# One core, a planned schedule: spread memsets, own weight tiles for two early products, another estimate for early transfers, systems in four transfers

## The chip, the cores and the metric

The kernel runs on 1 core of one Trainium2 chip. The metric is the time of one execution on the device in microseconds (us); lower is better. Comparisons are of medians of several runs.

## The reference

One layer of an encoder trunk on a prompt of 2048 tokens (width 1024) and a sample of 32 tokens with a cache. A combined projection feeds two branches, chunk-band attention (A) and a gated delta rule (B); both are gated, projected, merged and normalised.

```python
h = layer_norm(x, ln0_g, ln0_b)
qa, ka, va, za, qkv_b, zb, a_b, b_b, gate_a, gate_b = split_projection(h @ w_in)
ya = (chunk_band_attention(qa, ka, va, rel_bias) * silu(za)) @ w_branch_a
c = silu(causal_conv(qkv_b, conv_w));  qb, kb, vb = split(c)          # l2-normalised q and k
# per block of 64 tokens and head:
m = (k_beta @ kb.T) * decay * strict
t_inv = triangular_solve(eye + m, eye)                               # the "system"
u = t_inv @ v_beta;  w = t_inv @ (k_beta * exp(gc))
v_new = u - w @ s;  o = (q * exp(gc)) @ s + qk @ v_new               # recurrence over blocks
s = s * exp(g_last) + k_dec.T @ v_new
yb = (rms_norm(o) * silu(zb)) @ w_branch_b
y  = layer_norm(ALPHA * h + (sigmoid(gate_a) * ya + sigmoid(gate_b) * yb) @ w_out)
```

## The kernel before

**Precision and products.** Everything is float32. A product of the combined projection multiplies 128 columns of `w_in` with the normalised input, kept transposed in `hT`. Both sides are split into a half-precision part and its rest (`hi`, `lo` of the input, `whi`, `wlo` of the weights), so a block of 512 tokens takes 3 x 8 matmuls of 128x512: `whi` and `wlo` on `hi`, then `whi` on `lo`. They go to the two PSUM banks `pj`; an `evac` of each block copies the result on.

**Stages.** The 2048 tokens are worked on in two halves. For each half the products of branch B run first, then those of branch A; the gates' products fill in between. The order of the first half's products (`all_jobs`): two gates (`HEAD`), which are called products 1 and 2 here; the small product of the columns a and b (`w_ab`, 64 columns), product 3; then the convolution channels of the first pair of heads, products 4, 5 and 6, and so on; six gates (`TAIL`) close branch B's phase, and then comes branch A with its values (`vf`). Products 1 and 2 run together (`two`): their blocks of 256, 256 and 512 tokens alternate.

**The way of a weight.** `fetch` loads the raw weights into one of two tiles `wraw` (gate `raw_gate`). `divide` takes a `w_gate`, of which there are two, and with it a pair `whi`, `wlo`; the sum of squares of the weights (ACT, a small matmul `b<-w_sq` on PE, then DVE, POOL and DVE: `power`) gives a scale; ACT scales and casts, POOL subtracts. `multiply` gives the `w_gate` back behind the last block of a product.

**The way of the input.** `build_h` loads 16 tiles of 128 tokens; a tile takes statistics and a normalisation on DVE, eight transposes on PE into banks `b` and `a`, scaling on ACT and DVE, a cast on ACT (`hi`) and a subtraction on POOL (`lo`). The first 8 tiles are the first half.

**Branch B.** `phase_b` makes block-diagonal matrices (`diag`): 4 tiles `k_bd`, 4 `qk_bd`, 3 each of `q_bd`, `kd_bd`, `u_bd`, 128x1024 each, set to zero on DVE where they are made, once for each half. `worker` does the convolutions, `prep` the decays, `system` the matrices of one block of a pair of heads (8 chunks at once); it writes the systems to DRAM (`sol_p`). `solve` reads them back into `sys_p`, with one system on each row, the four groups of 32 rows holding the same 128 KB, and `substitute` solves them on DVE in 31 steps. `inverse` puts the result together, and `chain` runs the recurrence, whose matmuls go to banks `x` and `o`: 64 steps in the first half, in each of which PE and DVE take turns (`r`, `vn`, `state`).

**What sets the order.** The program is one stream of instructions for each engine. It is not written by hand: generators (`Stream`) yield at gates and marks, and a planner (`Flow`) always continues the one with the smallest planned clock. Each instruction adds a planned cost (`price`), each transfer a planned landing (`transfer`). An engine does its instructions strictly in the order so found; all that the planner estimates can change is this order. Every compute instruction is recorded at line 260 and every transfer at line 283, so the profile's rows are told apart by the names of tiles.

```python
        start = max(self.cur.clock + 0.2, self.busy.get(queue, 0.0)) + 0.5
        self.busy[queue] = start
        end = max(start + 0.6, self.busy.get("DMA", 0.0)) + size / 200e3
```

Of the kernel before, what the change touches and what calls it, by code (L numbers as in the profile page):

```python
# [56 lines left out]
for _p in range(1, NP):  # L57
    ORDER += [(_p, 0), (_p, 1), (_p, 2), (_p - 1, 3)] + [None] * FILL[_p]
ORDER += [(NP - 1, 3)]
MARGIN = 1.6  # L60
LEAD = 5.0
BLOCKS = [
    [(0, 512, 0), (512, 512, 512)],
    [(0, 512, 1024), (512, 272, 1536), (784, 272, 1808)],
# [90 lines left out]
class Flow:  # L155
# [47 lines left out]
    def transfer(self, queue, size):  # L203

        start = max(self.cur.clock + 0.2, self.busy.get(queue, 0.0)) + 0.5
        self.busy[queue] = start
        end = max(start + 0.6, self.busy.get("DMA", 0.0)) + size / 200e3
        self.busy["DMA"] = end
        return end + MARGIN

# [58 lines left out]
def trunk(ctx: ExitStack, tc: tile.TileContext, x_p, x_s, cache_k, cache_v, st_conv, st_gdn,  # L269
# [301 lines left out]
    class Job:  # L571
# [3 lines left out]
        def __init__(self, half, wid, src, evac=None, key=None, cols=P, blocks=None):  # L575
            self.wid = wid
            self.half, self.src, self.evac, self.cols, self.key = half, src, evac, cols, key
            self.end = self.two = False
            self.blocks = blocks or BLOCKS[half]

    NRAW = 2
# [41 lines left out]
    def divide():  # L623

        while True:
            job, raw, t = yield from q_raw.get()
            yield w_gate
            hi = wpool.tile([P, KD, P], F16, tag="whi", bufs=2, name="whi")
            lo = wpool.tile([P, KD, P], F16, tag="wlo", bufs=2, name="wlo")
            sc = w_scale[:, job.wid:job.wid + 1]  # L630
            yield t
            if job.half == 0:
                S.activation(out=hi[:], in_=raw[:], func=AF.Square, accum_out=w_sq[:])

                yield flow.cur.clock + (0.0 if job.wid < 34 and job.wid > 31 else 1.0)
                yield from power(sc, w_sq[:])
                flow.start(factors(job.wid))
            src, main = raw[:, :, 0:job.cols], hi[:, :, 0:job.cols]
            S.activation(out=src, in_=src, func=AF.Copy, scale=sc)
            for i in range(2):  # L640
                ks = slice(4 * i, 4 * i + 4)
                S.copy(out=main[:, ks], in_=src[:, ks])
                yield

                rest_ = lo[:, ks] if job.cols == P else hi[:, ks, job.cols:P]
                for q in range(0, 4, 2):
                    G.tensor_tensor(out=rest_[:, q:q + 2], in0=src[:, 4 * i + q:4 * i + q + 2],
                                    in1=main[:, 4 * i + q:4 * i + q + 2], op=ALU.subtract)
                if i:
                    raw_gate.give()  # L650
                    q_w.put((job, hi, lo))
                yield
# [14 lines left out]
    def multiply():  # L667

        while True:
            some, todo = [], [(0, 0)]  # L670
            while todo:
                bi, which = todo.pop(0)
                if which == len(some):
                    some.append((yield from q_w.get()))
                    job = some[which][0]
                    if which == 0:

                        todo = [(b, w) for b in range(len(job.blocks)) for w in range(1 + job.two)][1:]
                    if job.key:
                        job.open = mark()  # L680
                        flow.start(open_job(job))
                job, wh, wl = some[which]
                c0, n, gcol = job.blocks[bi]
                tiles = range(c0 // P, (c0 + n + P - 1) // P)
                for i in tiles:
                    yield h_ready[job.half][i]
                hh, hl = h_cols(job.half, c0, n)
                yield bank["pj"]
                ps = pt("pj")
                for k in range(KD):  # L690
                    PE.matmul(ps[:, 0:n], wh[:, k], hh[:, k, :], start=(k == 0), stop=False)
                    yield
                    if job.cols == P:
                        PE.matmul(ps[:, 0:n], wl[:, k], hh[:, k, :], start=False, stop=False)
                        yield
                for i in tiles:
                    yield l_ready[job.half][i]
                for k in range(KD):
                    PE.matmul(ps[:, 0:n], wh[:, k], hl[:, k, :], start=False, stop=(k == KD - 1))
                    if k == KD - 1:  # L700
                        last = bi == len(job.blocks) - 1
                        if job.end and (bi == 0 or last):
                            h_free[0 if bi == 0 else 1].give()
                        if last:
                            w_gate.give()
                    yield
                flow.start(evac(job, bi, c0, n, gcol, ps))
                if job.end and job.half == 1:
                    if last:
                        jobs_done.done()  # L710
                        flow.start(leave())
# [74 lines left out]
    def phase_b(half):  # L786
# [21 lines left out]
        def diag(name, bufs):  # L808
            ts = []
            for i in range(bufs):  # L810
                t = bp.tile([P, 8, P], F32, name=f"{name}{i}")
                V.memset(t[:], 0.0)
                ts.append(t)
            return ts

        k_bd, qk_bd = (diag(n, NPAR) for n in ("k_bd", "qk_bd"))
        q_bd, kd_bd, u_bd = (diag(n, NSIDE) for n in ("q_bd", "kd_bd", "u_bd"))
# [353 lines left out]
        def system(k):  # L1171
# [3 lines left out]
            k.par = yield from par_slots.take()  # L1175
            yield k.qk_ready
            yield k.prep
            k.pn = yield from p_slots.take()
            kb, qkb = k.kb, k.qkb = k_bd[k.par], qk_bd[k.par]
            p_c = k.p_c = p_cs[k.pn]  # L1180
# [44 lines left out]
        def solve():  # L1225
            while True:
                k, t = yield from q_sys.get()
                sys_p = bp.tile([P, 32, 32], F32, tag="sys_p", bufs=2, name="sys_p")
                sys_u = bp.tile([P, 8, 32], F32, tag="sys_u", bufs=2, name="sys_u")
                sys_t = bp.tile([P, 8, 32], F32, tag="sys_t", bufs=2, name="sys_t")  # L1230
                G.memset(sys_u[:], 0.0)
                for g in range(4):
                    G.memset(sys_u[g * 32:(g + 1) * 32].rearrange("p r i -> p (r i)")[:, g::36], 1.0)
                yield t
                p0 = pd[k.n % (2 * NP)][:]
                yield dma(sys_p[:].rearrange("p j i -> p (j i)"),
                          bass.AP(p0.tensor, p0.offset, [[0, 4], [1024, 32], [1, 1024]]))
                yield from substitute(sys_p, sys_u, sys_t)
                for g in range(4):
                    t = dma(ud[k.n % (2 * NP)][:].rearrange("s (r g i) -> g s r i", g=4, i=32)[g], sys_u[g * 32:(g + 1) * 32])  # L1240
                flow.start(inverse(k, t))
# [191 lines left out]
                return job_ab()  # L1433
            return job_conv(p, i) if i < 3 else job_z(p)

        for g in (worker(todo), worker(decays), prep(), local(), solve(), solve()):
            flow.start(g)
        for some in blocks + ([[sample]] if last else []):
            flow.start(chain(some))
# [504 lines left out]
    def marked():  # L1944

        ahead, half = [], None
        for job in all_jobs():
            if job.half != half:
                if ahead:
                    ahead[-2].two = ahead[-1].end = True  # L1950
                    yield from ahead
                ahead, half, n = [], job.half, 0
                job.two = True
            n += 1
            if n <= 2:
                if job.key is None:
                    job.blocks = FIRST[half]
                yield job
                continue
            ahead.append(job)  # L1960
            if len(ahead) > 2:
                yield ahead.pop(0)
        ahead[-2].two = ahead[-1].end = True
        yield from ahead
# [258 lines left out]
            all_done.done()  # L2223


    with ExitStack() as stack0:
        open_banks(stack0, "ps0", a=3)
        xp = stack0.enter_context(tc.tile_pool(name="x0", bufs=1, reuse_waits="tile"))
        flow.start(norm_params(xp))
        flow.start(build_h(0, xp, 8))  # L2230
        flow.start(fetch(marked()), 2.0)
        flow.start(setup(xp), 20.0)
        flow.start(setup2(xp), 30.0)
        flow.start(spread(), 100.0)
        flow.start(divide())
        flow.start(multiply())
        flow.run(l_ready[0][7])
    for half in range(2):
        stack, make, done = phase_b(half)
        enter(1, half, make)  # L2240
        flow.run(done)
        stack.close()
        if half:
            wr_pool.append(ctx.enter_context(tc.tile_pool(name="wr0", bufs=1)))
            wr_open.done()
            gp = ctx.enter_context(tc.tile_pool(name="gp", bufs=1, reuse_waits="tile"))
            for gen in (load_g(), sg_ahead(), merge()):
                flow.start(gen)
# [67 lines left out]
```

## Time and profile before

| what | value |
|---|---|
| median of 3 runs | 2083.18 us (2080.98 to 2087.81) |
| the profiled execution | 2081.13 us |
| its span | 2079.4 us |
| mean granted clock of TensorE | 0.982 |
| DVE busy | 1456.5 us (70%) |
| ACT busy | 977.0 us (47%) |
| POOL busy | 709.3 us (34%) |
| moved by DMA | 196.53 MB, mean 95 GB/s |

The profile is of one execution. PE is the matmul engine, DVE the vector engine, ACT the scalar engine, POOL the general engine, SP the queue that issues all transfers. In a row of the timeline stand the start and the duration in us, the engine, the line, the operation, what it writes and reads, and in brackets how long the engine had been idle and what ended that. In a row of a table of windows stand, for each engine, its busy time and the number of its instructions, then the granted clock of PE, the share of the 16 DMA engines that was busy, and GB/s.

### The profile page before, as it was taken

What the parts mean: (1) busy time and instruction counts of PE and PEld (TensorE: products, weight loads), DVE (VectorE), ACT (ScalarE), POOL (GpSimd) and SP (SyncE); (2) the same over time, 40 slices, a digit from 0 to 9 for tenths busy, and PEclk for the clock granted to TensorE, in tenths of its full rate; (3) what the DMA queues carried; (4) which work ended last, traced back from release to release, by engine and by line L of the source; (5) the groups of instructions that cost most, each with busy time, mean ns of one, the idle gap of its engine ahead of it and who ended that gap; (6) DMA issues with size and microseconds to landing.
All of it is one profiled execution on the core that took longest, in us unless ns stands there. A gap on an engine that the chain in (4) does not pass through costs nothing. (4 is left out here: it accounts for less than half of the span.)

```text
span 2079.4 us, 41810 instructions
## 1 busy us (share of the span) xinstructions
PE 1969.9 (95%) x15098; PEld 1419.4 (68%) x15098; DVE 1456.5 (70%) x4673; ACT 977.0 (47%) x2098; POOL 709.3 (34%) x1075
## 2 busy tenths in 40 slices
PE   4899999999999999899999899999999999999998
PEld 3455666667465666566677676767667678999996
DVE  7579888874267667768998887347657677655565
ACT  5565645444466668564544434346566642111110
POOL 5254443423322123334333323311110224644443
PEclk9899999999999999999999999999999999999999
DMA  3132332232323333222233233332332345433331
GB/s 109 62 98 80 98 107 65 82 82 87 121 68 122 92 87 101 66 72 73 78 85 88 73 91 95 97 91 76 87 89 82 108 139 196 135 105 113 111 123 48
DMA packets 197724, 196.53 MB, mean 95 GB/s; under 512 B 79623, under 2 KB 147571, under 8 KB 197517
## 3 DMA queue, kind: packets, MB, share of 16 engines
q1 hardware_dynamic: 197516, 193.85, 31.7%
q8 instruction: 119, 1.95, 0.4%
q14 instruction: 89, 0.72, 0.1%
HBM read 135.91 MB, written 50.53 MB: 90 GB/s over the span
## 5 line engine op out<-in xcount | busy, mean ns | idle before, releaser
L260 PE MATMUL pj<-hi,whi 128*128 128x512 f16 (+2 forms) x1992 | 654.3, 344 | 12.6 <-POOL whi L260 2.4
L260 PE MATMUL pj<-hi,wlo 128*128 128x512 f16 (+2 forms) x1952 | 644.4, 342 | 2.0 <-POOL wlo L260 1.9
L260 PEld LDWEIGHTS <-whi 128*128 128x128 f16 x3984 | 412.7, 105 | 222.2 <-issue 11.1
L260 PE MATMUL pj<-lo,whi 128*128 128x512 f16 (+2 forms) x1992 | 461.3, 339 | 0.0
L260 POOL TENSOR_TENSOR wlo<-wraw,whi 128x256 f16<-128x256 f32 x384 | 263.8, 708 | 570.9 <-ACT whi L260 328.4
L260 PEld LDWEIGHTS <-wlo 128*128 128x128 f16 x1952 | 207.1, 106 | 112.6 <-issue 11.2
L260 ACT CAST mh<-sg 128x256 fp32r<-128x256 f32 x64 | 26.0, 407 | 273.7 <-DVE sg L260 273.7
L260 ACT ACTIVATE wraw<-wraw,w_scale 128x1024 f32<-128x1024 f32 (+1 forms) x98 | 111.5, 1138 | 64.9 <-DVE w_scale L260 51.9
L260 ACT CAST ph<-b 128x512 f16<-128x512 f32 (+2 forms) x224 | 92.9, 422 | 100.2 <-PE b L260 95.4
L260 PE MATMUL a<-ghi,whi 128*128 128x256 f32 (+1 forms) x512 | 132.5, 290 | 4.9 <-DVE sg L260 4.7
L260 DVE TENSOR_TENSOR pl<-b,ph 128x512 f16<-128x512 f32 (+2 forms) x224 | 107.2, 485 | 37.9 <-ACT ph L260 36.8
L260 PE MATMUL a<-ghi,wlo 128*128 128x256 f32 (+1 forms) x512 | 130.6, 286 | 1.1 <-DVE wlo L260 1.1
L260 ACT CAST whi<-wraw 128x512 f16<-128x512 f32 (+1 forms) x196 | 119.6, 611 | 23.4 <-PE pj L260 20.5
L260 DVE TENSOR_TENSOR sys_u<-sys_u,sys_t 128x60 f32<-128x60 f32 (+24 forms) x527 | 123.3, 240 | 6.1
L260 POOL TENSOR_TENSOR w_scale<-w_scale,mhalf 128x1 f32<-128x1 f32 x49 | 32.4, 662 | 257.0 <-DVE w_scale L260 204.0
L260 ACT ACTIVATE sb<-sb,mx,unit 128x640 f32<-128x640 f32 (+4 forms) x128 | 108.8, 851 | 20.7 <-DVE mx L260 20.3
L260 DVE SCALAR_TENSOR_TENSOR acc<-raw,cwT,acc 128x512 f32<-128x512 f32 x144 | 112.0, 777 | 5.2 <-ACT acc L260 4.1
L260 DVE TENSOR_TENSOR sys_t<-sys_u,sys_p 128x60 f32<-128x60 f32 (+20 forms) x459 | 111.2, 246 | 5.9
L260 PEld LDWEIGHTS a<-ghi,whi 128*128 128x128 f32 x512 | 98.2, 192 | 7.3 <-DVE sg L260 7.0
L260 ACT COPY v_t<-o 128x64 f32<-128x64 f32 x132 | 27.6, 209 | 157.0 <-PE o L260 113.1
L260 PE MATMUL b<-ident,sb 128*128 128x128 f32 x560 | 99.3, 277 | 1.9 <-DVE ga L260 0.9
L260 PEld LDWEIGHTS a<-ghi,wlo 128*128 128x128 f32 x512 | 97.8, 191 | 1.9 <-DVE wlo L260 1.6
(350 smaller groups left out, 4237.0 us busy)
## 6 DMA issues: line engine op xcount, KB each, us to landing
wraw<-in_w_in SPq DMA_DIRECT2D x192, 256.0 KB
sg<-sig SPq DMA_DIRECT2D x112, 128.0 KB
sig<-sig SPq DMA_DIRECT2D x44, 256.0 KB
sys_p<-sol_p SPq DMA_DIRECT2D x17, 512.0 KB
x<-in_x_p SPq DMA_DIRECT2D x16, 512.0 KB
xt<-in_x_p SPq DMA_DIRECT2D x16, 512.0 KB
out_y_p<-xt SPq DMA_DIRECT2D x16, 512.0 KB
glo<-g SPq DMA_DIRECT2D x14, 512.0 KB
```

What stands on the lines that cost most here:

```text
L260: r = f(*a, **k)
```

## The change

Four things are changed.

1. The 17 memsets of the block-diagonal matrices are issued by a stream of their own, `zeros`, which waits a planned 1.2 us behind each; `system` waits for its mark `zeroed`.
2. Products 3 and 4 of the first half get weight tiles of their own (`first_w`: `whi3`; `whi4`, `wlo4`) and neither take nor give a `w_gate`. The pool closes behind the first half's branch B.
3. The planner takes 360 instead of 200 KB per us for transfers that start before a planned 25 us.
4. `sys_p` is loaded with four transfers of 32 rows, one for each group, in place of one whose source begins with a dimension of 4 and stride 0.

```diff
+ZERO = 1.2
...
-        end = max(start + 0.6, self.busy.get("DMA", 0.0)) + size / 200e3
+        end = max(start + 0.6, self.busy.get("DMA", 0.0)) + size / (360e3 if start < 25.0 else 200e3)
...
             self.end = self.two = False
+            self.own = None
...
             job, raw, t = yield from q_raw.get()
-            yield w_gate
-            hi = wpool.tile([P, KD, P], F16, tag="whi", bufs=2, name="whi")
-            lo = wpool.tile([P, KD, P], F16, tag="wlo", bufs=2, name="wlo")
+            if job.own:
+                hi, lo = job.own
+            else:
+                yield w_gate
+                hi = wpool.tile([P, KD, P], F16, tag="whi", bufs=2, name="whi")
+                lo = wpool.tile([P, KD, P], F16, tag="wlo", bufs=2, name="wlo")
...
-                        if last:
+                        if last and not job.own:
                             w_gate.give()
...
                 t = bp.tile([P, 8, P], F32, name=f"{name}{i}")
-                V.memset(t[:], 0.0)
                 ts.append(t)
             return ts
+        zeroed = mark()
+        def zeros():
+            for t in [t for some in (k_bd, qk_bd, q_bd, kd_bd, u_bd) for t in some]:
+                V.memset(t[:], 0.0)
+                yield flow.cur.clock + ZERO
+            zeroed.done()
...
             yield k.prep
+            yield zeroed
             k.pn = yield from p_slots.take()
...
-                yield dma(sys_p[:].rearrange("p j i -> p (j i)"),
-                          bass.AP(p0.tensor, p0.offset, [[0, 4], [1024, 32], [1, 1024]]))
+                for g in range(4):
+                    t = dma(sys_p[g * 32:(g + 1) * 32].rearrange("p j i -> p (j i)"),
+                            bass.AP(p0.tensor, p0.offset, [[1024, 32], [1, 1024]]))
+                yield t
...
-        for g in (worker(todo), worker(decays), prep(), local(), solve(), solve()):
+        for g in (zeros(), worker(todo), worker(decays), prep(), local(), solve(), solve()):
...
+            if half == 0 and 2 < n <= 4:
+                job.own = [first_w.tile([P, KD, P], F16, name=f"{x}{n}") if x == "whi" or job.cols == P else None
+                           for x in ("whi", "wlo")]
+            if half == 0 and n == 3:
+                yield job
+                continue
             if n <= 2:
...
+    stack_w = ExitStack()
+    first_w = stack_w.enter_context(tc.tile_pool(name="first_w", bufs=1, reuse_waits="tile"))
...
         stack.close()
+        stack_w.close()
```

The instructions are the same in number and kind, but for the transfers of `sys_p` (68 for 17). Their order changes on every engine. Three places follow.

PE, from the first sum of squares (`b<-w_sq`) to the first matmul of product 1 (`pj`); `x0` to `x4` are tiles of the input, `prm` is a tile of parameters. Before:

```order
L260 MATMUL b_305<-w_sq_127,tiny_125 128x1
L260 MATMUL a_315<-ident_106,x3_160 128x128 x4
L260 MATMUL b_326<-ident_106,x3_160 128x128 x4
L260 MATMUL b_370<-ident_106,x4_170 128x128 x4
L260 MATMUL a_375<-ident_106,x4_170 128x128 x4
L260 MATMUL b_401<-ident_106,prm_283 128x85
L260 LDWEIGHTS whi_165
L260 MATMUL pj_412<-hi00_150,whi_165 128x256
```

And now:

```order
L262 MATMUL b_244<-w_sq_127,tiny_125 128x1
L262 MATMUL b_250<-ident_106,x1_159 128x128 x4
L262 MATMUL a_255<-ident_106,x1_159 128x128 x4
L262 MATMUL b_277<-ident_106,x2_161 128x128 x4
L262 MATMUL a_297<-ident_106,x2_161 128x128 x4
L262 MATMUL b_325<-ident_106,x3_163 128x128 x4
L262 MATMUL a_335<-ident_106,x3_163 128x128 x4
L262 MATMUL b_366<-ident_106,prm_303 128x85
L262 LDWEIGHTS whi_168
L262 MATMUL pj_379<-hi00_153,whi_168 128x256
```

The sum of squares moved from behind the third tile to behind the first, and the transposes of `x4` no longer stand ahead of product 1.

ACT, around the steps that make the weights of products 3 and 4: `sig` are the copies of the blocks of products 1 and 2 (128x512 the third one), `w_sq` marks a sum of squares, `ab` is product 3's result. Before, `whi_728` is product 3's weight tile and `whi_780` product 4's:

```order
L260 ACTIVATE sig_700<-pj_674,w_half_130 128x256
L260 ACTIVATE whi_728,w_sq_127<-wraw_408 128x1024
L260 ACTIVATE sig_731<-pj_702,w_half_130 128x512
L260 ACTIVATE sig_762<-pj_733,w_half_130 128x512
L260 ACTIVATE wraw_408<-wraw_408,w_scale_128 128x8x64
L260 CAST whi_728<-wraw_408 128x4x64 x2
L260 ACTIVATE whi_780,w_sq_127<-wraw_546 128x1024
L260 ACTIVATE ab_804<-pj_783,w_inv_129 40x512
L260 ACTIVATE wraw_546<-wraw_546,w_scale_128 128x1024
L260 CAST whi_780<-wraw_546 128x512
```

And now, from product 3's last cast on (its sum of squares stands twelve rows further up):

```order
L262 ACTIVATE sig_648<-pj_615,w_half_130 128x256
L262 CAST whi3_173<-wraw_375 128x4x64
L262 ACTIVATE whi4_430,w_sq_127<-wraw_500 128x1024
L262 ACTIVATE sig_742<-pj_651,w_half_130 128x512
L262 ACTIVATE wraw_500<-wraw_500,w_scale_128 128x1024
L262 CAST whi4_430<-wraw_500 128x512 x2
L262 ACTIVATE sig_782<-pj_744,w_half_130 128x512
L262 ACTIVATE whi_801,w_sq_127<-wraw_721 128x1024
L262 ACTIVATE ab_812<-pj_784,w_inv_129 40x512
```

Product 3's weights are finished ahead of the first copy of a third block, and product 4's ahead of the second one; product 5's sum of squares (`whi_801`) stands ahead of product 3's result.

SP, at the first load of `sys_p`; `gcb` are decays, `ext_dram` rows of the bias table. Before:

```order
L283 DMA wraw_1360<-in_w_in 128x512 x2
L283 DMA sig02_70<-sig_1356 128x512
L283 DMA sys_p_1293<-sol_p00_614 128x1x1024
L283 DMA wraw_1497<-in_w_in 128x512 x2
L283 DMA ext_dram3_93<-ext_row_89 128x768
```

And now:

```order
L285 DMA sol_p00_688<-p_c0_704 32x8x32 x4
L285 DMA wraw_1425<-in_w_in 128x512 x2
L285 DMA gcb_1440<-gc_dram_88 64x512 x2
L285 DMA sys_p_1390<-sol_p00_688 32x1024 x4
L285 DMA wraw_1559<-in_w_in 128x512 x2
```

One issue of 128 rows became four of 32, and it stands behind the next decays' loads.

## The prediction

> **What bounds the kernel now.** I read the page first, then a table of windows, then the timeline and the waits of TensorE (PE).
>
> ```profile
> span 2079.4 us, 41810 instructions
> PE 1969.9 (95%) x15098; PEld 1419.4 (68%) x15098; DVE 1456.5 (70%) x4673; ACT 977.0 (47%) x2098; POOL 709.3 (34%) x1075
> ```
> PE is busy for 1969.9 of 2079.4 us, so 109.5 us is all that the removal of idle time could give; beside it stand matmuls at a lower clock.
>
> ```profile
> core 0: us, PE busy (x) PEld busy (x) DVE busy (x) ACT busy (x) POOL busy (x), PEclk, DMA share, GB/s
> 0.00:10.00 10.00, 1.07 (x4) 0.94 (x5) 5.86 (x25) 1.28 (x1) 1.80 (x8) 1.00 0.75 268
> 24.00:54.00 30.00, 16.69 (x82) 12.12 (x83) 24.89 (x60) 18.82 (x40) 22.70 (x26) 0.92 0.10 21
> 60.00:103.00 43.00, 35.75 (x205) 17.01 (x204) 21.93 (x46) 25.67 (x38) 12.91 (x21) 0.89 0.16 52
> 103.00:110.00 7.00, 7.00 (x26) 3.13 (x25) 3.82 (x13) 2.53 (x4) 1.76 (x3) 0.69 0.38 107
> 200.00:550.00 350.00, 335.03 (x2503) 224.74 (x2502) 256.80 (x1001) 167.19 (x345) 133.51 (x218) 0.98 0.32 89
> ```
> The loss is dense at the start. From 24 to 54 us DVE and POOL are the busy engines (24.89 and 22.70 of 30 us): they normalise the tiles of x. From 60 to 103 us nobody is full, and PE still idles 7.3 us. Between 200 and 550 us PE idles 15.0 of 350 us.
>
> ```profile
> 30.00 1.11 PE L260 MATMUL b<-ident,x 128*128 128x128 f32 x4 [6.76 <-DVE x L260]
> 31.90 0.42 PE L260 MATMUL pj<-hi,whi 128*128 128x256 f16 x1
> 51.59 2.28 POOL L260 TENSOR_TENSOR lo<-tmp,hi 128x512 f16<-128x512 f32 x2
> 60.38 0.38 PE L260 MATMUL pj<-hi,whi 128*128 128x512 f16 x1
> 60.59 0.38 PE L260 MATMUL pj<-hi,wlo 128*128 128x512 f16 x1
> 65.76 1.06 ACT L260 ACTIVATE whi<-wraw 128x1024 f16<-128x1024 f32 x1 [4.66 <-PE pj L260]
> 73.47 3.40 PE L260 MATMUL pj<-hi,whi 128*128 128x512 f16 x8 [2.43 <-POOL whi L260]
> 89.35 0.84 PE L260 MATMUL b<-ident,ab 40*64 40x40 f32 x22 [1.73 <-DVE ab L260]
> 100.72 1.93 PE L260 MATMUL b<-ident,ab 40*64 40x40 f32 x32 [2.56 <-DVE ab L260]
> 102.59 0.61 PE L260 MATMUL pj<-hi,whi 128*128 128x512 f16 x1
> 102.99 0.63 PE L260 MATMUL pj<-hi,wlo 128*128 128x512 f16 x1
> ```
> Products are numbered as in the section on the kernel: 1 and 2 (gates) run together, 3 is a/b, 4 and 5 are the first convolution ones. The third block of products 1 and 2 starts at 60.38, though its last rest `lo` was there at 53.87 (51.59 + 2.28). Product 3's first step on ACT (65.76) waited for PE, that is for product 1 to give its weight tile back; so its weights came late (2.43 us at 73.47), product 4's after them, and the two decays that hang on product 3 were late too (1.73 and 2.56 us). Product 5 starts at 102.59. A 128x512 matmul steps by 0.21 us at 60.38 and by 0.40 at 102.59: after such idle time PE runs at half rate.
>
> **The early products.** This edit adds no work to PE; it removes waits. What PE has from the third block to product 5: 48 matmuls of products 1 and 2, 32 of product 3, 48 of product 4, together 128 x 0.216 (the step at full rate, 60.38 to 60.59) = 27.6 us, with 0.84 for the first decay (89.35) and some 0.6 for sums of squares 29 us. In the profile it takes 42.2 (60.38 to 102.59). With weight tiles of their own, products 3 and 4 are split while PE works on the third block, as the ACT rows in the section on the change show, and the second decay comes behind product 5.
>
> When can the third block start? Not before the last `lo`. The planner's higher rate for early transfers puts four instead of five tiles of x ahead of the first product. A tile costs DVE about 4 us:
>
> ```profile
> 6.60 0.68 DVE L260 BATCH_NORM_STATS2 st<-x 128x6 f32<-128x512 f32 x1
> 8.82 0.80 DVE L260 TENSOR_SCALAR x<-x,mv 128x1024 f32<-128x1024 f32 x1
> 11.75 0.73 DVE L260 TENSOR_SCALAR tmp<-a,ln0gT,ln0bT 128x128 f32<-128x128 f32 x2 [1.22 <-PE a L260]
> ```
> (2 x 0.68 + 0.80 + 2 x 0.73, and some 0.4 of small ones). So the first product starts near 28 instead of 31.9. Its 96 narrow matmuls at half rate (0.21 us) take 20.4 us, the four tiles left 4 x 1.9 us of transposes (30.00 to 31.76 is one with its copy of parameters): 28 + 28 = 56 us; the sum of work on DVE and POOL is the same, so 53.9 is the floor. On SP the first store of `sig` now stands ahead of the load of `rr`, whose copies on DVE stand ahead of two tiles of x; that store waits for the first block's end, and up to 2 us of DVE may go there, inside these 54 to 56. Third block at 54 to 56, product 5 at 83 to 85: 17.6 to 19.6 us earlier. Bounds: if only the waits behind 60.38 go, 60.38 + 29 = 89.4, a gain of 13.2; if it all starts 2 us below the floor, 21.6. **I take -17.5.** Product 5 no longer starts behind an idle PE: 7 us at a clock of 0.69 give 7 x 0.31 = 2.2, **-2** (bounds 0 and 2.2).
>
> **The spread memsets.**
> ```profile
> 47.68 0.91 DVE L260 MEMSET k_bd<- 128x1024 f32 x1 [0.16 <-issue]
> 64.86 0.91 DVE L260 MEMSET u_bd<- 128x1024 f32 x1 [0.16 <-issue]
> 880.93 1.13 PE L260 MATMUL b<-ident,ab 40*64 40x40 f32 x32 [1.63 <-DVE ab L260]
> ```
> 17 memsets of 1.07 us (0.91 + 0.16) stay, in each half; they leave one block and go between DVE's other steps. In the first half nothing stood behind the block (product 3 waited for its tile), so the move itself is worth 0; what hides them is DVE's idle time, 21 of 43 us from 60 to 103. Without it each holds up a step that PE waits for by up to 1.07 us, 18 us in all. The new wait `zeroed` stands ahead of the first system; behind it on DVE is the copy into `k_bd`, and the order has all 17 ahead of it anyway. In the second half PE waits 1.63 us soon after the block; **-1** (bounds -3 and +2).
>
> **The systems in four transfers.**
> ```profile
> 143.00:149.50 6.50, 6.50 (x44) 3.68 (x44) 3.91 (x13) 4.39 (x8) 5.54 (x9) 1.00 0.27 95
> 437.48 0.24 DVE L260 TENSOR_SCALAR sys_t<-sys_p,sys_u 128x31 f32<-128x31 f32 x1 [4.25 <-DMA sys_p<-sol_p]
> 438.06 0.44 PE L260 MATMUL x<-r,u_bd 128*128 128x64 f32 x2 [3.43 <-DVE r L260]
> 1195.00 0.24 DVE L260 TENSOR_SCALAR sys_t<-sys_p,sys_u 128x31 f32<-128x31 f32 x1 [4.83 <-DMA sys_p<-sol_p]
> 1195.48 0.69 PE L260 MATMUL x<-state,k_bd 128*128 128x64 f32 x2 [4.48 <-DVE state L260]
> 440.00:445.00 5.00, 4.90 (x29) 3.65 (x28) 3.11 (x18) 2.61 (x5) 1.34 (x2) 0.82 0.20 37
> 1195.00:1200.00 5.00, 4.51 (x23) 3.54 (x24) 2.93 (x17) 1.38 (x3) 0.00 (x0) 0.55 0.38 116
> 141.26 0.63 SPq L283 DMA_DIRECT2D sys_p<-sol_p x1
> ```
> While the 512 KB of `sys_p` arrive, a quarter of the 16 DMA engines is busy (0.27) at 95 GB/s: 5.5 us. The loads of the first 10 us use three quarters of them at 268 GB/s, where 512 KB take 2.0 us. SP has three issues more per system (up to 0.63 us each, 1.9 us, part of it under the first transfers), so some 3 us are saved each time. Twice the load held up DVE (4.25, 4.83) and PE behind it (3.43, 4.48), and the clock fell (0.82 and 0.55 of 5 us, 3.1 us). All that PE lost there is 11 us; **I take -8**, bounds 0, since other rows may become the late ones, and -11.
>
> The Trainium skill ("DMA: Bandwidth & Descriptors", "Rules for kernel authors") says that a leading zero-stride broadcast of c copies confines a transfer to at most c engines; the 0.27 agrees. The same page speaks against the edit: under "Anatomy of one DMA" it gives each transfer (issued from GpSimd; these are SP's) a fixed cost of about 2.0 us, and under "Bandwidth" it wants them batched to 1 MiB. An estimate by that page, if the four came one after another: 4 x 2.3 = 9.2 us, against 3.2 for one. The trace's first loads, issued in a row, speak for overlap.
>
> **What the new order costs elsewhere.** The order of every engine differs from the first tile of x to the end of the second half's attention. PE's waits from 200 to 550 us are 15 us: the new order may lose or gain as much. In the order the last matmul of the first half's recurrence comes behind 1,449 of the 1,472 product matmuls of its phase, before behind 1,379.
>
> ```profile
> 507.86 0.28 DVE L260 SCALAR_TENSOR_TENSOR r<-x,negc,v_t 128x64 f32<-128x64 f32 x1 [0.53 <-PE x L260]
> 510.30 0.29 DVE L260 SCALAR_TENSOR_TENSOR r<-x,negc,v_t 128x64 f32<-128x64 f32 x1 [0.53 <-PE x L260]
> 512.10 0.28 DVE L260 SCALAR_TENSOR_TENSOR state<-state,sc,x 128x64 f32<-128x64 f32 x1 [0.50 <-PE x L260]
> 537.15 0.69 ACT L260 ACTIVATE vf<-pj,w_inv 128x512 f32<-128x512 f32 x1 [3.54 <-PE pj L260]
> ```
> Before, 93 product matmuls (20 us) fill the 25 us from the recurrence's end to attention's first copy; now 23 (5 us). PE can go two blocks further (10 us) into two banks, so some lead may be spent there. **I take +4** (bounds -15 and +15).
>
> Sum: -17.5 - 2 - 1 - 8 + 4 = -24.5. The profiled execution took 2081.13 us (span 2079.4), the median is 2083.18, 2 us more: 2083.2 - 24.5 = **2058.7 us**.
>
> **The rivals.**
> 1. Only the start gains, the rest keeps its waits: -17.5 - 2 + 4, 2068 us. For it: 15 of the 17 loads of `sys_p` show no long wait.
> 2. The lead is given back: the recurrence ends no earlier than now, and attention waits for it. Then the gain is what PE finds to do, 70 x 0.216 = 15 us, less waits of up to that: 2083 us, no change.
> 3. Slower: the recurrence of the first half. It has 64 steps, each with three turns between PE and DVE (one alone takes 2.44 us, 507.86 to 510.30), and PE, in order, stands behind each turn. The products now come some 20 us earlier, so more of DVE's other work lies between the turns. If that adds more than 24.5 / 64 = 0.4 us to every step, the whole gain is gone; at 0.6 us it is 64 x 0.6 - 24.5 = +14, 2097 us. Against it: DVE idles 93 of the 350 us.
> 4. The four transfers come one after another, and each takes as long as the 512 KB at the first loads' rate, 2.0 us: 8 us, 2.5 later than now; the two places lose 5 us instead of gaining 8: 2072 us. (This is what the skill's fixed cost would do.)
> 5. The own tiles do nothing, since the weights arrive late anyway: the 13.2 us behind 60.38 stay, 2072 us. Against it: ACT waited for PE at 65.76, not for a DMA.
>
> **How the numbers follow.** Forecast 0.52, rival 1 0.18, rival 2 0.08, rival 3 0.08, rival 4 0.06, rival 5 0.08. The range 2040 to 2077 takes in the start's bounds and most of the 15 us on either side, and leaves out rivals 2 and 3 and the tails. About 0.3%, 6 us, is what a measurement can tell. Faster is the forecast with rivals 1, 4 and 5 (0.84), less 0.02 for its upper tail: 0.82; same is rival 2, that tail and a little of rival 3, 0.11; slower the rest of rival 3, 0.07.
>
> **What would show it.** Right: product 5's first matmul near 84 us; no wait of over 2 us for `whi` or `ab` before 110; a DMA share well above 0.27 while `sys_p` lands, and no wait of 4 us for it. Wrong: DVE's steps of the recurrence at more than 2.8 us, PE waiting for `vf` or `vs` behind the first half, or product 5 later than 90.

## The result, and the profile after

| kernel | median | range, runs | ratio to before, 95% interval |
|---|---|---|---|
| before | 2083.44 us | 2080.98 to 2087.81, 4 | |
| after | 2055.95 us | 2055.24 to 2059.20, 4 | 0.9864 [0.9846, 0.9883] |

The change saves 27.5 us in the medians and 25.9 us in the profiled spans (2079.4 to 2053.5). The forecast was 2058.7. First the page's head and the table of windows of the kernel after, for the same stretches as in the prediction:

```profile
span 2053.5 us, 41889 instructions
PE 1963.6 (96%) x15098; PEld 1417.4 (69%) x15098; DVE 1454.8 (71%) x4673; ACT 976.5 (48%) x2098; POOL 712.9 (35%) x1075
```
```profile
core 0: us, PE busy (x) PEld busy (x) DVE busy (x) ACT busy (x) POOL busy (x), PEclk, DMA share, GB/s
24.00:54.00 30.00, 24.77 (x157) 17.91 (x155) 18.85 (x56) 21.10 (x48) 25.02 (x30) 1.00 0.21 56
60.00:103.00 43.00, 42.92 (x258) 20.82 (x257) 32.12 (x63) 29.54 (x43) 16.13 (x27) 1.00 0.19 60
103.00:110.00 7.00, 6.35 (x39) 3.12 (x38) 4.35 (x13) 6.16 (x11) 3.03 (x5) 1.00 0.28 97
200.00:550.00 350.00, 335.65 (x2498) 223.64 (x2496) 256.66 (x1002) 165.25 (x342) 132.32 (x220) 0.98 0.34 93
```
Two things are to be seen. The start is cured: from 60 to 103 us PE is busy for 42.92 of 43 us (before 35.75), and the clock is 1.00 in all three early windows (before 0.92, 0.89, 0.69). The clock's record begins at 36.93 us here and at 42.42 before, and a window counts what lies ahead of it as 1.00; the rows of 0.42 us below show half rate until then. Between 200 and 550 us nothing is won: PE idles 14.3 us there, before 15.0. Now the rows of PE's timeline that answer to those of before:

```profile
23.16 0.42 PE L262 MATMUL pj<-hi,whi 128*128 128x256 f16 x1
...
36.63 0.42 PE L262 MATMUL pj<-hi,whi 128*128 128x256 f16 x1
...
37.00 0.27 PE L262 MATMUL pj<-hi,whi 128*128 128x256 f16 x1
...
48.61 0.38 PE L262 MATMUL pj<-hi,whi 128*128 128x512 f16 x1 [0.69 <-ACT hi L262]
...
75.74 1.13 PE L262 MATMUL b<-ident,ab 40*64 40x40 f32 x32
...
77.81 0.38 PE L262 MATMUL pj<-hi,whi 128*128 128x512 f16 x1
...
88.26 1.13 PE L262 MATMUL b<-ident,ab 40*64 40x40 f32 x32
```
The third block of products 1 and 2 starts at 48.61 (before 60.38), product 5 at 77.81 (102.59), and both decays (the `ab` rows) start without a wait.

**How far ahead the kernel is, by place.** The orders differ, so that two times in two traces don't stand for the same work. One number compares them all the same: each matmul on PE counts with the median of the time that it adds (matmuls overlap; by tile and shape, over the 14 profiles of this study, before and after among them), and PE's *loss* at a place is the time less the work done so far; the sum runs to the last matmul. The work is some 1906 us in all; 60 us of it are done at about 112 us before and 86 us after.

| kernel | loss up to 60 us of work | 60 to 700 | 700 to 1110 | rest | sum |
|---|---|---|---|---|---|
| before | 52.1 | 29.3 | 40.9 | 43.1 | 165.3 |
| after | 26.2 | 29.1 | 41.8 | 42.1 | 139.2 |

The first column is the start, the second the rest of the first half's branch B and all of its branch A, the third the second half's branch B. All of the gain stands in the first column: 25.9 us. Behind it the two kernels lose alike, though the waits for `sys_p` are gone. So, as far as one execution of each can tell, something behind the start took what the four transfers gave; the experiments look for it.

### The profile page after: what moved, and what is told of

It reads as the page before. It is cut to its first block, busy times and chain, and to the rows that moved or that the text cites. A ratio compares the mean times of both kernels' runs of the same rounds, so it can differ in the third digit from the quotient of the medians.

```text
span 2053.5 us, 41889 instructions
## 1 busy us (share of the span) xinstructions
PE 1963.6 (96%) x15098; PEld 1417.4 (69%) x15098; DVE 1454.8 (71%) x4673; ACT 976.5 (48%) x2098; POOL 712.9 (35%) x1075
## 5 line engine op out<-in xcount | busy, mean ns | idle before, releaser
L262 PE MATMUL pj<-hi,whi 128*128 128x512 f16 (+2 forms) x1992 | 647.2, 340 | 12.0 <-ACT sig L262 3.2
L262 PEld LDWEIGHTS <-wlo 128*128 128x128 f16 x1952 | 205.7, 105 | 112.9 <-issue 10.7
L262 ACT ACTIVATE wraw<-wraw,w_scale 128x1024 f32<-128x1024 f32 (+1 forms) x98 | 111.6, 1139 | 58.5 <-DVE w_scale L262 54.3
L262 DVE TENSOR_TENSOR sys_u<-sys_u,sys_t 128x60 f32<-128x60 f32 (+23 forms) x527 | 125.4, 242 | 7.8
L262 DVE TENSOR_TENSOR pl<-b,ph 128x512 f16<-128x512 f32 (+2 forms) x224 | 106.9, 484 | 30.4 <-ACT ph L262 29.3
L262 DVE TENSOR_TENSOR sys_t<-sys_u,sys_p 128x60 f32<-128x60 f32 (+21 forms) x459 | 111.4, 244 | 6.5
```

The source lines that it names most:

```text
L262: r = f(*a, **k)
```

## The experiments

Each run was compared with runs of the kernel before on the same chip; its medians there were 2081.58 to 2084.93 us. Every difference below is against the one beside which the run was made.

**split_only** and **one_load**: the transfers of `sys_p` alone. To keep the order, the planner is charged as it was.

The diff is that of split_only against before; one_load undoes this edit in the kernel after, and charges the planner for four.

```diff
-                yield dma(sys_p[:].rearrange("p j i -> p (j i)"),
-                          bass.AP(p0.tensor, p0.offset, [[0, 4], [1024, 32], [1, 1024]]))
+                for g in range(4):
+                    nc.sync.dma_start(sys_p[g * 32:(g + 1) * 32].rearrange("p j i -> p (j i)"),
+                                      bass.AP(p0.tensor, p0.offset, [[1024, 32], [1, 1024]]))
+                yield flow.transfer("SP", P * 1024 * 4)
```


> The kernel before with sys_p in four transfers and nothing else; the order on PE, DVE, ACT and POOL is that of before. Theory A (all of the 26 us came from the start, the four transfers are worth nothing): 2083 us, within 3 us of before; DVE's waits for sys_p at 437 and 1195 us shrink, but PE then waits there for other rows. Theory B (the four transfers are worth the 8 us forecast, and the new order of the change gave them back): 2073 to 2076 us, PE's waits of 3.43 us (r) and 4.48 us (state) gone. Theory C (rival 4, one transfer after another): 2086 to 2088 us. A and B both expect a DMA share well above 0.27 while sys_p lands.

> The kernel after with sys_p again in one transfer; the order on PE, DVE, ACT and POOL is that of after. Theory A: 2056 us, within 3 us of after. Theory B: 2060 to 2066 us, with waits of 2 to 5 us for sys_p on DVE at one or more of the 17 systems, and PE behind them. Theory C: 2051 to 2053 us.

split_only took 2071.46 us, 10.7 less than before; ratio 0.9953 [0.9934, 0.9972]. one_load took 2062.00 (0.99 [0.9874, 0.9926]), some 4 to 6 more than the kernel after took in its own comparisons; its interval meets that of after_again below (0.9857 to 0.9904). The table of windows, while the first `sys_p` lands, of one_load and then of after:

```profile
126.00:128.00 2.00, 2.00 (x14) 1.17 (x13) 1.93 (x5) 0.29 (x2) 0.00 (x0) 1.00 0.68 245
128.00:130.00 2.00, 2.00 (x11) 0.94 (x10) 1.92 (x5) 0.86 (x2) 1.12 (x2) 1.00 0.18 54
130.00:132.00 2.00, 2.00 (x11) 0.93 (x10) 1.20 (x5) 1.97 (x3) 0.35 (x1) 1.00 0.26 102
132.00:134.00 2.00, 1.57 (x16) 0.86 (x14) 1.20 (x2) 1.80 (x4) 1.07 (x3) 1.00 0.23 96
134.00:136.00 2.00, 2.00 (x16) 1.15 (x15) 1.92 (x5) 0.00 (x0) 2.00 (x3) 1.00 0.04 14
```
```profile
127.00:129.00 2.00, 2.00 (x15) 1.26 (x13) 1.68 (x3) 0.63 (x3) 0.00 (x0) 1.00 0.88 287
129.00:131.00 2.00, 2.00 (x11) 0.92 (x10) 1.92 (x7) 0.63 (x1) 1.12 (x2) 1.00 0.92 261
131.00:133.00 2.00, 2.00 (x11) 0.88 (x9) 1.57 (x6) 1.83 (x3) 0.00 (x0) 1.00 0.15 35
```
The one transfer creeps along at a quarter of the engines (0.18 to 0.26) and 54 to 102 GB/s until 134; the four use nine tenths of them, at 261 to 287 GB/s, and are there by about 131.5. So 8 us became 4. In split_only the two long waits of before are gone; the loss from 60 to 1110 us of work falls from 70.2 to 64.0. (Its first column is 4.6 us better as well, ahead of the first system, where nothing differs: that much comes from one execution to another.) Theory B comes nearest (split_only is 1.5 us below its range): the four transfers are worth about 6 to 11 us in the order of before and, less surely, 4 to 6 in that of after, and theory C (rival 4) is out. One sign of theory B is missing: one_load's waits of DVE for `sys_p` are 0.92, 0.23 and 1.15 us long, not 2 to 5, so that they explain only a part of its 4 to 6 us.

**own_only** and **rate_only**: the own weight tiles alone (its order differs from before only at a few places near 60 us, and not at all on DVE), and the planner's estimate alone.

First the core of own_only's diff against before, then rate_only's.

```diff
-            yield w_gate
-            hi = wpool.tile([P, KD, P], F16, tag="whi", bufs=2, name="whi")
-            lo = wpool.tile([P, KD, P], F16, tag="wlo", bufs=2, name="wlo")
+            if job.own:
+                hi, lo = job.own
...
-                        if last:
+                        if last and not job.own:
                             w_gate.give()
```
```diff
-        end = max(start + 0.6, self.busy.get("DMA", 0.0)) + size / 200e3
+        end = max(start + 0.6, self.busy.get("DMA", 0.0)) + size / (360e3 if start < 25.0 else 200e3)
```


> The kernel before with own weight tiles for products 3 and 4 and nothing else. The order on DVE and SP is that of before, PE, ACT and POOL differ near 60 us alone. Theory A (own tiles remove the 13.2 us of loss behind 60.38 by themselves): product 5 at 89 to 91 us, 2070 us. Theory B (the block of 17 memsets on DVE, 47.7 to 65.8 us, stands ahead of product 3's scale, so that own tiles gain only the wait for product 1): product 5 at 96 to 100 us, 2077 to 2081 us. Theory C (rival 5): product 5 at 102 to 103, 2083 us.

> The kernel before with 360 in place of 200 KB per us for early transfers and nothing else. In all theories the first product starts near 23 us and the third block of products 1 and 2 near 49 us. Theory A (the estimate's 12 us at the third block arrive at product 5): product 5 at 90 to 92 us, 2071 us. Theory B (they are lost in the wait for the weights of products 3 and 4, since product 1's tile and the memsets on DVE set these): product 5 at 97 to 102 us, 2078 to 2083 us.

own_only took 2084.83 us (1.0009 [0.9991, 1.0028]), rate_only 2093.50 (1.0062 [1.0038, 1.0086]): the two edits that I had expected to carry the gain give nothing, and a loss of 11 us, when they stand alone. The rows of own_only's timeline (ACT, DVE, ACT, and PE with `pj` and `ab`) say why:

```profile
51.43 1.05 ACT L260 ACTIVATE whi<-wraw 128x1024 f16<-128x1024 f32 x1
```
```profile
64.84 0.91 DVE L260 MEMSET u_bd<- 128x1024 f32 x1 [0.16 <-issue]
65.66 0.10 DVE L260 TENSOR_SCALAR w_scale<-b 128x1 f32<-128x1 f32 x1
```
```profile
71.31 0.69 ACT L260 ACTIVATE sig<-pj,w_half 128x512 f32<-128x512 f32 x1 [4.49 <-PE pj L260]
71.89 0.71 ACT L260 ACTIVATE wraw<-wraw,w_scale 128x512 f32<-128x512 f32 x1
```
```profile
73.66 3.52 PE L260 MATMUL pj<-hi,whi 128*128 128x512 f16 x8 [2.43 <-POOL whi L260]
...
100.93 1.93 PE L260 MATMUL b<-ident,ab 40*64 40x40 f32 x32 [2.45 <-DVE ab L260]
102.80 0.61 PE L260 MATMUL pj<-hi,whi 128*128 128x512 f16 x1
```
The own tile does what it should: ACT's first step of product 3 runs at 51.43, not at 65.76 behind a wait for PE. But the scale, DVE's next step in that chain, stands behind the 17 memsets and comes at 65.66; and ACT takes it up only at 71.89, behind a copy of `sig` that waits for PE. PE waits the same 2.43 us as before. Theory A of own_only falls; product 5 (102.80) is where theory C had it, and the block of theory B is one of two reasons. In rate_only the third block does start at 47.44, but PE then waits 8.12 us for product 3's weights, and product 5 comes at 94.69, between the places of its two theories. Its time is 10 us above both: between 60 and 700 us of work it loses some 49 us, where before loses 29. The edit changes nothing but the order, so that this is a price of the order.

**no_zeros**, **no_own**, **no_rate**, **zeros_only**: the kernel after without one of its edits each, and the spread memsets alone.

The diff is the core of no_zeros against after (the wait for `zeroed` goes too); the reverse of it, in before, is zeros_only, and no_own and no_rate undo the edits of the two diffs above.

```diff
                 t = bp.tile([P, 8, P], F32, name=f"{name}{i}")
+                V.memset(t[:], 0.0)
                 ts.append(t)
...
-        for g in (zeros(), worker(todo), worker(decays), prep(), local(), solve(), solve()):
+        for g in (worker(todo), worker(decays), prep(), local(), solve(), solve()):
```


> The kernel after with the 17 memsets in one block again. Theory A (the memset block gates product 3's scale on DVE, so own tiles need the spread): product 3's first matmul at 65 to 67 us instead of 59.1, PE waiting 6 to 8 us there, product 5 at 84 to 87 instead of 77.8; 2063 to 2066 us if the rest keeps its order's worth, and up to 10 us either way for the new order. Theory B (own tiles alone are enough, as the prediction had it: the spread is worth nothing in the first half): product 3 at 59 to 60, product 5 at 78 to 79, 2056 us.

> The kernel after without own weight tiles. Product 3's first step on ACT waits for product 1's tile, back near 52.8 us. Theory A (with the memsets out of the way the chain of scale and split, some 7.7 us, ends near 60.5): product 3 at 60 to 62, product 4 at most 3 us late, product 5 at 80 to 83; 2058 to 2062 us. Theory B (own tiles are worth the 13 us that the prediction gave them): product 5 at 88 to 91 us, 2067 to 2070 us.

> The kernel after with the old estimate of 200 KB per us. Theory A (the estimate brings the third block 12 us forward and nothing else; own tiles and spread memsets bring the 13 us behind it): third block at 60 to 61 us, product 5 at 89 to 91, 2066 to 2070 us. Theory B (the later stages set the end, the start does not): 2056 to 2060 us. Theory C: product 5 at 100 or later, 2076 to 2082 us.

> The kernel before with the memsets spread and nothing else. Theory A (product 3 then waits for product 1's tile alone): product 3 at 72 to 74 us, product 5 at 100 to 103, so no gain at the start, and 2076 to 2090 us by the new order. Theory B (the block alone was the gate): product 3 at 70.7, product 5 at 90 to 92, 2071 us.

The medians: no_zeros 2052.09 (0.9863 [0.9835, 0.9892]), no_own 2075.56 (0.9966 [0.9951, 0.9981]), no_rate 2071.54 (0.9954 [0.9939, 0.9969]), zeros_only 2078.64 (0.9985 [0.997, 1.0]). With these, all eight combinations of the three edits that bear on the start are there (no_zeros, no_own, no_rate and after have the four transfers too, which come later than product 5):

| own tiles | spread | estimate | kernel | third block | product 5 | between |
|---|---|---|---|---|---|---|
| | | | before | 60.38 | 102.59 | 42.2 |
| x | | | own_only | 60.70 | 102.80 | 42.1 |
| | x | | zeros_only | 60.83 | 103.59 | 42.8 |
| | | x | rate_only | 47.44 | 94.69 | 47.3 |
| x | | x | no_zeros | 47.36 | 88.98 | 41.6 |
| | x | x | no_own | 47.51 | 90.28 | 42.8 |
| x | x | | no_rate | 60.00 | 89.21 | 29.2 |
| x | x | x | after | 48.61 | 77.81 | 29.2 |

The estimate sets when the third block starts, and 13 us are won between it and product 5 only where own tiles **and** spread memsets are there. PE's rows of no_zeros, no_own and zeros_only at product 5, and then of no_rate, show where they go:

```profile
87.12 1.93 PE L261 MATMUL b<-ident,ab 40*64 40x40 f32 x32 [5.00 <-DVE ab L261]
88.98 0.61 PE L261 MATMUL pj<-hi,whi 128*128 128x512 f16 x1
```
```profile
88.42 1.93 PE L262 MATMUL b<-ident,ab 40*64 40x40 f32 x32 [6.47 <-DVE ab L262]
90.28 0.61 PE L262 MATMUL pj<-hi,whi 128*128 128x512 f16 x1
```
```profile
101.73 1.93 PE L261 MATMUL b<-ident,ab 40*64 40x40 f32 x32 [8.14 <-DVE ab L261]
103.59 0.61 PE L261 MATMUL pj<-hi,whi 128*128 128x512 f16 x1
```
```profile
89.21 0.38 PE L262 MATMUL pj<-hi,whi 128*128 128x512 f16 x1
...
99.66 1.06 PE L262 MATMUL b<-ident,ab 40*64 40x40 f32 x29
```
In the first three, as in before, the second decay stands ahead of product 5 on PE, and PE waits for its `ab` and goes on at half rate (a decay of 32 takes 1.93 us, not 1.13). With its wait, its own 1.13 us and the half rate until product 5, the decay makes up some 7 of the 12.4 us that no_zeros needs more than the kernel after between the third block and product 5, and some 5 of the 13 in before. The rest is waits for the weights of products 3 and 4 (2.96 us in both) and for the first decay (0.48 and 1.73), with the half rate behind them. With both edits the planner puts product 5 ahead of it. The decay comes no sooner for that: DVE's last step for it, a scan, starts at 85.40 in no_zeros and at 86.25 in after:

```profile
85.40 1.57 DVE L261 TENSOR_TENSOR_SCAN ab<-reset,row 8x512 f32<-8x512 f32 x1
```
```profile
86.25 1.21 DVE L262 TENSOR_TENSOR_SCAN ab<-reset,row 8x512 f32<-8x512 f32 x1
```
PE merely has a product to do meanwhile. Both theories of no_own miss in part: product 3 is in time, as A had it, product 5 where B had it, and the whole is slower than either said, by 18 to 20 us against after. In no_zeros theory A had the place wrong (product 3 starts at 57.85; PE waits 2.60 us for product 4 and 5.00 for the decay), and product 5 at 88.98 is even later than A said. Yet the kernel is no slower than the kernel after: 12 us of lead at the start don't show at the end. no_rate and zeros_only have their third block and product 5 about where their theories A had them, with 2 us more than A's range in the one and a time inside it in the other.

**after_again**, **spread_first**, **spread_second**: whether the spread is worth anything, and in which half. With no_zeros they are the four kernels that differ in the memsets alone.

The diff is spread_first against after; spread_second has `half == 1`.

```diff
                 t = bp.tile([P, 8, P], F32, name=f"{name}{i}")
+                if not (half == 0):
+                    V.memset(t[:], 0.0)
                 ts.append(t)
...
-                V.memset(t[:], 0.0)
-                yield flow.cur.clock + ZERO
+                if half == 0:
+                    V.memset(t[:], 0.0)
+                    yield flow.cur.clock + ZERO
```


> The kernel after, run beside the two that follow. 2053 to 2058 us. If it is no slower than the kernel with its memsets in one block (2052.09 us measured), the spread is worth nothing in sum; if it stays near 2056, the spread costs some 4 us in sum.

> The kernel after with the memsets spread in the first half and in one block in the second. Theory A (the spread costs the second half's branch B some 6.6 us, from PE's loss between 700 and 1110 us of its work: 41.8 us with the spread, 35.2 with the block, and its gain in the first half stays): 2048 to 2051 us, the best of all. Theory B (the two halves' shares are accidents of one run): 2055 to 2058 us.

> The kernel after with the memsets in one block in the first half and spread in the second. Theory A: 2057 to 2062 us, the slowest of the four kernels that differ in the memsets alone. Theory B: 2052 to 2056 us.

| kernel | spread in | median | ratio to before | loss to 60 | 60 to 700 | 700 to 1110 | rest |
|---|---|---|---|---|---|---|---|
| after_again | both halves | 2057.88 | 0.988 [0.9857, 0.9904] | 26.1 | 28.2 | 45.2 | 41.9 |
| spread_first | the first | 2055.79 | 0.9863 [0.9834, 0.9891] | 26.0 | 32.3 | 35.8 | 45.2 |
| spread_second | the second | 2058.55 | 0.9882 [0.9857, 0.9906] | 39.0 | 18.4 | 43.0 | 41.5 |
| no_zeros | neither | 2052.09 | 0.9863 [0.9835, 0.9892] | 38.0 | 22.0 | 35.3 | 45.6 |

The intervals overlap: as a whole, the spread can't be told from nothing. The columns show two effects. In the first half the spread is 12 us ahead at 60 us of work, and from there to 700 the kernels with the block lose less (18.4 and 22.0 against 28.2 to 32.3). What is lost up to 700 is then 54.3, 55.3 (after) and 58.3 us with the spread, 57.4 and 60.0 with the block: about 3 us are left in the mean, less than the 4 by which kernels with the same first half differ. In the second half the spread costs 7 us or more in these kernels (43.0 and 45.2, and 41.8 in after, against 35.3 and 35.8), as theory A said; but the rest takes 3 us back, and the time of spread_first shows 2 of the 7 and not the 2048 to 2051 us of theory A. In the other traces the two overlap: in this stretch before, with the block, loses 40.9 and rate_only some 43, other_order, with the spread, some 39. So the order may do it as well, and whether the block in the second half is the better choice stays open.

**other_order**: another order and nothing else.

```diff
-MARGIN = 1.6
+MARGIN = 1.5
```


> The kernel after with the planner's MARGIN at 1.5 in place of 1.6 us, which leaves PE's order as it is until 154 us and gives another order behind it, with no other change. Theory A (the order of branch B's two phases, which no edit sets on purpose, is worth up to 10 us either way, as PE's loss between 60 and 700 us of its work, 18 to 49 us in the kernels so far, suggests): product 5 at 78 us again, PE's loss between 60 and 700 us of its work more than 3 us away from after's 29, and a time more than 5 us away from 2056 to 2058 us, on either side. Theory B (these differences come from the edits themselves): 2054 to 2060 us.

It took 2064.38 us (0.9909 [0.9888, 0.993]), 6.5 to 8.4 more than the kernel after. Product 5 is at 76.41, so the start is the same; from 60 to 700 us of work PE loses 43.4 us instead of 29.1. A row of PE's timeline and a row of windows from the place where the first half's recurrence ends:

```profile
525.02 0.58 PE L262 MATMUL pj<-hi,whi 128*128 128x512 f16 x1 [4.34 <-ACT vf L262]
```
```profile
520.00:525.00 5.00, 0.38 (x2) 0.32 (x3) 1.81 (x8) 3.15 (x7) 1.55 (x3) 0.82 0.46 117
```
PE does 0.38 us of work in 5, waiting for a copy of `vf`. Theory A holds: 0.1 us in one of the planner's numbers moves the time by as much as the four transfers do (its interval is clear of that of the kernel after, and overlaps a little with that of after_again).

**What the runs leave open.** Why a lead of 12 us at the start is evened out by 700 us of work, by a limit of branch B or by the chance of the order, was not settled; nor was why the planner chooses product 5 ahead of the decay only with both edits. No kernel here is measurably faster than the kernel after.

## Why the prediction was right

The total was right (-24.5 forecast, -25.9 between the profiled executions, -27.5 in the medians), because two misses cancel, and that is luck: the start gave 25.9 us where 19.5 were forecast (17.5 and 2), and all that lies behind it gave nothing where 5 were.

- **The third block (54 to 56 us forecast, 48.61 measured): the start of the first product and the step "53.9 is the floor" failed.** The first product starts at 23.16, not near 28. The prediction took off the 4 us that a tile of x costs DVE; but its own row at 30.00 says that PE had been idle for this tile for 6.76 us, since 23.24, and up to 31.90 that is 8.7. The floor was read from before: the last `lo` itself is done at 49.80 now (48.64 + 1.16) instead of 53.87, and the block begins ahead of it. It starts with 16 matmuls on `hi` alone (16 x 0.216 = 3.5 us), and waited 0.69 us for ACT's `hi`. The 96 narrow matmuls at half rate, 20.4 us in the sum, were at half rate only until about 36.8: from 37.00 on the rows are 0.27 us long instead of 0.42. That is the smaller part: one_load and other_order, with the same order here, are at full rate from about 31, and their third block starts at 47.25 and 47.21. The memsets set nothing here: rate_only has them in one block, and its third block starts at 47.44. The term of -17.5 should have been -24.8.
- **From the third block to product 5 (29 forecast, 29.2 measured): right, but put down to the wrong edit.** I gave it to the own tiles and wrote that the spread in the first half "itself is worth 0", since nothing stood behind the block. That was read from before, where product 3 waited for its tile; with that wait gone, product 3's scale is what stands behind it (65.66 in own_only). What I named in passing, "the second decay comes behind product 5", is some 5 us of the 13 against before and some 7 against no_zeros, and it takes both edits. Alone, the tiles come to what rival 5 said, though the weights were late for their scale, not for their load.
- **Half rate, -2: right.** In the clock's record PE had 20.5 us at half rate between 42.42 and 110 us before, and from 36.93 to 110 none after. (Ahead of that it was at half rate in both.)
- **The spread in the second half, -1 (bounds -3 and +2): not borne out** (some +7 between 700 and 1110 us of work in the four kernels above), though little of it is seen in the times, and the order may do it as well.
- **The four transfers, -8: mechanism right, size 6 to 11 in the order of before, 4 to 6 in that of after.** I estimated some 3 us saved on each load; it is 4. The share of the DMA engines while they land is 0.88 to 0.92. The rule of the Trainium skill ("DMA: Bandwidth & Descriptors", "Rules for kernel authors") on a leading zero stride agrees: 0.18 to 0.26 with it. The same page's fixed cost, by which four small transfers would have taken 9.2 us in the prediction's estimate, didn't show: from the first issue to the end they took 4.
- **The new order, +4 (bounds -15 and +15): right in kind.** Behind the start the losses are 113.2 before, 113.0 after and 115.3 in after_again; so what the transfers gave was spent there. other_order shows that 15 was a fair bound: 14 us between 60 and 700.
- **The rivals.** Rival 1's picture (only the start gains) is what came out, with a larger start than it had. Rival 2's place was real, but in another order: 4.34 us for `vf` in other_order; in after no wait for `vf` or `vs` around the recurrence's end is above 0.8. Rival 3: the recurrence did become longer. Its last `state` of the first half is at 502.08 (512.10 before) after a start at 204.5 (233.8), 0.3 us more for each of the 64 steps; its price wasn't paid. That PE had products to do in them is the likely reason; no run tests it.

The last `lo` of the first half's input, on POOL, and the last `state` of its recurrence, on DVE:

```profile
48.64 1.16 POOL L262 TENSOR_TENSOR lo<-tmp,hi 128x512 f16<-128x512 f32 x1
```
```profile
502.08 0.28 DVE L262 SCALAR_TENSOR_TENSOR state<-state,sc,x 128x64 f32<-128x64 f32 x1 [0.53 <-PE x L262]
```

## What to carry to other kernels

In a planned schedule an edit's worth is not a property of the edit: the same own tiles gave 0 alone and some 19 us with the others, and a change of 0.1 us in one planner number gave 7 by itself, so a gain of 10 us in such a kernel should be tested with the order held still (as in split_only) and beside another order. When a wait is taken away, follow the same chain to its next step, on every engine, and ask what stands ahead of it there; here it was the memset block. Ask of a lead at the start what is left of it at the end of the phase: it was 12 us at 60 us of work and about 3 at 700.

## What the runs showed of the hardware

A wait of two to three microseconds often costs PE more than itself. The row is PE's, the windows are of the kernel after:

```profile
207.94 0.66 PE L262 MATMUL x<-r,u_bd 128*128 128x64 f32 x2 [2.46 <-DVE sys_t L262]
```
```profile
208.00:210.00 2.00, 2.00 (x9) 1.82 (x10) 0.59 (x3) 0.00 (x0) 0.00 (x0) 0.50 0.68 243
210.00:212.00 2.00, 2.00 (x10) 1.71 (x9) 1.20 (x4) 0.21 (x1) 0.00 (x0) 0.50 0.96 289
212.00:214.00 2.00, 2.00 (x9) 1.17 (x9) 1.82 (x6) 0.00 (x0) 0.31 (x1) 0.50 0.11 25
214.00:216.00 2.00, 2.00 (x13) 1.18 (x12) 1.89 (x7) 0.13 (x1) 0.38 (x2) 0.90 0.00 0
```
After 2.46 us of waiting the clock stays at 0.50 for some 6.4 us, which costs 3.2 more. Over the 14 traces (behind 40 us), the clock fell, at the latest 1.5 us behind the wait's end, with 45 of 62 waits of 2 to 3 us, 14 of 15 longer ones, and 37 of 224 of 1 to 2 us; it fell for 3.4 us or a multiple of that, but for the stretch at the program's end. The Trainium skill ("TensorE: Matmul & The Clock Gate", "Part 1: The HAM clock gate (the "warmup" mystery)") gives idle windows of about 3.4 us as what brings the half clock: the step of 3.4 us agrees, but most waits of 2 to 3 us were enough here. Before had 76.3 us at half clock, after 52.5, and after_again, the same program, 66.0.
